# Value products kept together in fours with TensorE's order pinned, and fewer gathers at the ends of the mixings

## The chip, the cores and the metric

One NeuronCore of a Trainium2 chip runs the whole program. Its engines run beside each other, each through its own queue in order: TensorE (PE: matmuls, with its weight loads shown apart as PEld), VectorE (DVE), ScalarE (ACT), GpSimd (POOL) and SyncE (SP). DMAs are issued from the queues of SP, ACT and POOL. The metric is the device time of one execution in microseconds; lower is better.

## The reference

One inference step of a two-layer backbone, on 128 prompt tokens (context) and 256 latent tokens of width 1024, all in float32. A layer is a mixing (windowed attention, a bidirectional mLSTM and a pooling, between two projections) and then PEER, a feed-forward with 16384 experts of one row each, of which every token takes 16 for each of 8 heads:

```python
def trunk_layer(x, mods, p, ctx_kv, mlstm_init, rope_pos):
    h = rmsnorm(x, p['norm1_g']) * (1 + sc1) + sh1
    y, kv, fins = mixing_sublayer(h, p, ctx_kv, mlstm_init, rope_pos)
    x = x + g1 * y
    h = rmsnorm(x, p['norm2_g']) * (1 + sc2) + sh2
    x = x + g2 * peer_ffn(h, p['peer_wq'], p['peer_keys'], p['peer_u'], p['peer_v'])

def peer_ffn(x, w_q, sub_keys, u_table, v_table):
    s = jnp.einsum('thcd,hckd->thck', q, sub_keys).astype(F32)
    top_s, top_i = lax.top_k(s, PEER_TOPK)
    cand = (top_s[:, :, 0, :, None] + top_s[:, :, 1, None, :]).reshape(...)
    best_s, best_p = lax.top_k(cand, PEER_TOPK)
    ...
    a = jax.nn.gelu(jnp.einsum('thkd,td->thk', u_table[eb], xb), approximate=False)
    return jnp.einsum('thk,thkd->td', gb * a, v_table[eb])
```

## The kernel before

**Two ways through the experts.** The 256 latents take PEER densely: for all 16384 experts of a layer the up product, gelu, a weight from the routing, and the down product. The 128 prompt tokens take it sparsely: each token's 128 experts are gathered from memory.

**A layer's stages.** (1) The mixing, whose parts run in an order written out by hand, a string a layer (ORDER0, ORDER1). "route" in it routes the prompt's tokens; from there on their gathers can start. An entry "+n" advances the prompt's experts by n steps, one `next(pr.others)` each. (2) The latents' queries and scores: the normed latents (tile hw, written by VectorE in eight pieces), four groups of query products, and on VectorE the top 16 of each row (L937 to L941). ASKED tells how many of the prompt's steps go among these, by layer. (3) The latents' routing on VectorE, which ends in two index tiles ix for each 128 tokens, and 32 chunks of gate building (G) on VectorE, TensorE and ScalarE. Among these stand 23 dense up products ahead of their turn (L1087), and further steps of the prompt, paced by EARLY. The gates are written to memory and read back in parts (DMA gates<-stage, then G<-gates). (4) Dense.

**Dense.** 64 rounds, each over 256 experts (line 1115 on). A round issues the up product of 23 rounds later (rounds 0 to 40): two loads of 512 KB (tile u), each split into a high and a low half by ScalarE and VectorE, and 48 matmuls into A. Then `weigh` multiplies the round's gelu output with the gates, and `down` loads two tiles v, splits them likewise and issues 24 matmuls into po, the latents' accumulators. All these products are `mm3`: three passes (high x high, high x low, low x high). Loads go through a ring of 4 raw tiles. Then come as many of the prompt's steps as keep an even pace to the last rounds; a round with an up product counts double.

**The prompt's steps.** 259 a layer: 128 for keys, 128 for values, three more since work on a row lags its gather by three steps. A key step gathers one expert row for each token (tile gu, 512 KB, issued by GpSimd, L863), and three steps later VectorE takes the dot product with the tokens in one instruction (L883). A value step gathers two half rows (tile gv, twice 256 KB, L869), and every second value step issues a *four*: four products of 32 columns each, `q` = 0 to 3, into four 32-column groups of one PSUM bank pv (L896). Each is a float32 product, which stands as two instructions, so that a four is 8 instructions. The weights of a four are in a tile wz, which is made anew every 16 fours. Key and value rows share five gather buffers.

**What sets the order.** Python writes the instructions in program order, a scheduler then moves them by its estimates, within their dependences. `behind(m)` pins an instruction: it stays behind what was pinned earlier on its engine, in program order. It adds no wait. Before, pinned are each dot product (L883), the first of the four products of a four, the multiplication in `weigh`, one matmul of each chunk part of the gate build and the routing's transposes.

Of the kernel before, what the change touches and what calls it, by code (L numbers as in the profile page):

```python
# [22 lines left out]
KC = 8  # L23
# [13 lines left out]
ALSO = dict(t="at", q="at")  # L37
NRAW = 4

ORDER0 = "np ns kv c q gate qk ox | &mod1 mod1 mem2 mem0 mem1 att0 pool0 &mod2 att1 att2 pool1 mod2 &next0 mix0 spill norm ask mix1 next0 route +20 +3 +6 +3 +3"  # L40
ORDER1 = "np ns q c gate kv att0 qk ox &mod1 mod1 | mem0 pool0 &mod2 mod2 mix0 norm ask mem1 att1 spill route +5 +15 att2 mem2 pool1 +15 +10 mix1 +4"

BIAS = (1.0, 1.0)
NHI = 4
# [11 lines left out]
          dict(row=("r4", R4), PT=("r4", R4), half="half", P=("P", 2), W=("W", 1), num=("num", 1), hr=("hr", 1), hm=("hm", 1),  # L56
               quarter=("r1", 2)))

ASKED = (14, 0)
LAG = 3  # L60
END = (2, 3)
HEAD = 26.0
# [6 lines left out]
def tile_hybrid_step(ctx: ExitStack, tc: tile.TileContext, I, O):  # L69
# [29 lines left out]
        return t  # L99


    PASSES = ((0, 0), (0, 1), (1, 0))

    def split_into(hi, lo, src):
# [24 lines left out]
        split_into(hi, lo, raw)  # L129
        return hi, lo  # L130

    def mm3(out, a, b, first, last):
        for n, (x, y) in enumerate(PASSES):
            pe.matmul(out, a[x], b[y], start=first and n == 0, stop=last and n == 2, skip_group_check=True)  # L134

    class Room:

# [13 lines left out]
            return t  # L151

    GATH = Room(stay, row=("gath", NGATH), half="half", quarter="half")


    behind = tc.keep_in_program_order


    ident = ld("ident", [P, P], I["c_ident"], cst)
# [19 lines left out]
    def tsl(i):  # L179
        return slice(i * P, (i + 1) * P)  # L180
# [592 lines left out]
    class Prompt:  # L773
# [65 lines left out]
        def experts(self):  # L839
# [7 lines left out]
            for k in range(2 * P + LAG):  # L847
# [33 lines left out]
                if 0 <= j < P:  # L881
                    u = late.pop(j)
                    behind(ve.scalar_tensor_tensor(u, u, 1.0, self.h2n, op0=ALU.mult, op1=ALU.mult, accum_out=dots[:, j:j + 1]))  # L883
                elif j >= P and (j - P) % 2 == 1:
                    r, h = (j - P) // 4, (j - P) // 2 % 2
                    if r % 8 == 0 and h == 0:

                        wz = stay.tile([P, 8, 4, 32], F32, tag="row", bufs=1, name=f"wz{l}{r}")
                        gp.memset(wz, 0.0)
                        flat = wz.rearrange("p r j c -> p (r j c)")  # L890
                        for q in range(4):
                            at = 32 * q + r
                            ve.tensor_copy(flat[:, at:at + 7 * 129 + 1:129], wT[:, at:at + 8])  # L893
                    v = [late.pop(j - 1), late.pop(j)]
                    for q in range(4):
                        m = pe.matmul(self.acc[h][32 * q:32 * q + 32, :], wz[:, r % 8, q, :],  # L896
                                      v[q // 2][:, q % 2 * 512:q % 2 * 512 + 512], start=(r == 0), stop=(r == 31),
                                      skip_group_check=True)
                        if q == 0:
                            behind(m)  # L900
                yield

    def queries(l, most):
# [111 lines left out]
    class Experts:  # L1015
# [56 lines left out]
        def up(self, whole=None):  # L1072
# [7 lines left out]
            for j in range(2):  # L1080
                u = (load_split if whole is None else load_whole)(I["u_T"][l, 2 * bp + j], f"u{l}{bp}{j}")
                out = pa[:, j * 256:(j + 1) * 256]
                for k in range(KC):
                    if whole is None:
                        mm3(out, [t[:, tsl(k)] for t in u], [t[:, k, :] for t in self.hs], k == 0, k == KC - 1)
                    else:
                        pe.matmul(out, u[:, tsl(k)], whole[:, k, :], start=k == 0, stop=k == KC - 1, skip_group_check=True)  # L1087
            gl = self.lay.tile([P, 2, 2 * P], F32, tag="gl", bufs=LOOK[l] - 1, name=f"gl{l}{bp}")
# [13 lines left out]
        def down(self, po, bp, w):  # L1102
# [6 lines left out]
            for i, j in ((0, 0), (0, 1), (1, 0), (1, 1)) if end else ((0, 0), (1, 0), (0, 1), (1, 1)):  # L1109
                for h in range(2):  # L1110
                    mm3(po[i][h], [t[:, j, tsl(i)] for t in w], [t[:, h * 512:(h + 1) * 512] for t in v[j]],
                        bp == 0 and j == 0, end and j == 1)

    def dense(l, ex, p3, po, pr):

# [228 lines left out]
```

## Time and profile before

| | us |
|---|---|
| median of three runs | 2739.42 |
| lowest, highest | 2739.12, 2743.07 |
| the profiled execution | 2746.87 |
| its span | 2745.1 |
| TensorE, VectorE, ScalarE, GpSimd busy in it | 2500.7, 1722.4, 1045.5, 927.6 |
| dense, layer 0 | 683.0 to 1388.0 |
| dense, layer 1 | 2042.1 to 2732.1 |

The profile shows one execution, so its own time, and not the median, is what a sum over its rows is compared with. Busy shares are means over stages that differ much: TensorE is busy 91% of the span and full nearly everywhere in dense, but not at the ends of the scores. The chain of waits follows the work that ended last back to the beginning, and is where to see whether an engine, a transfer or a wait set the time of a stretch. The windows give the busy time of each engine in a stretch, and the DMA share and rate beside it.

### The profile page before, as it was taken

Reading aid. Unit: us, or ns where it says so; the run is one execution under the profiler, and the core shown is the slowest. Engines: PE = TensorE matmul, PEld = TensorE weight load, DVE = VectorE, ACT = ScalarE, POOL = GpSimd, SP = SyncE. Lnnn points to the kernel's source line nnn. Section 1 sums busy time; section 2 is a strip of 40 time slices with the busy share of each in tenths; the row PEclk is TensorE's granted clock in tenths of the full one; section 3 lists DMA queues with packets and bytes.
Section 4 is the critical chain, followed back from the end, with each engine's and each line's share of the span. In section 5 each row is a group of like instructions: output and inputs, shape, how many; then the busy total and the mean of one; then the engine's idle time right before and its main releaser. Section 6 shows DMA issues by size and latency. Waiting matters only on the chain.

```text
span 2745.1 us, 37514 instructions
## 1 busy us (share of the span) xinstructions
PE 2500.7 (91%) x13834; PEld 1915.5 (70%) x13834; DVE 1722.4 (63%) x3768; ACT 1045.5 (38%) x1545; POOL 927.6 (34%) x794
## 2 busy tenths in 40 slices
PE   7998779896999999999989885979969999999998
PEld 3744568785988777765666464868859877777665
DVE  4555979866877444443565468798778844444446
ACT  3434411544434433332444352114444433343333
POOL 0000034101445666754400002231224556656541
PEclk9998989897999999999999878999979999999999
DMA  7485589678899889897835644886999988888985
GB/s 258 139 269 194 167 289 337 210 268 321 305 352 347 303 314 330 290 330 259 292 122 166 218 162 152 315 291 232 334 347 353 329 296 311 299 315 289 330 294 192
DMA packets 217547, 749.33 MB, mean 273 GB/s; under 512 B 28308, under 2 KB 30868, under 8 KB 215316
## 3 DMA queue, kind: packets, MB, share of 16 engines
q1 hardware_dynamic: 137236, 444.91, 46.8%
q0 software_dynamic: 77824, 268.48, 27.9%
q10 hardware_dynamic: 2304, 33.56, 3.1%
q8 instruction: 108, 1.77, 0.3%
q14 instruction: 75, 0.61, 0.1%
HBM read 706.99 MB, written 39.85 MB: 272 GB/s over the span
## 4 chain that ended last, share of the span: by engine, by line
PE 62%; DMA 13%; DVE 12%; issue 7%; POOL 3%; ACT 2%; SPq 0%; POOLq 0%; DVEq 0%; ACTq 0%
PE po L134 22%; PE A L134 13%; PE pv L896 6%; DMA gu<-in_peer_u,ei 4%; PE A L1087 4%; PE pj_i L134 4%; DMA v_r<-in_peer_v 3%; DVE gu L883 3%; DMA gv<-in_v_half,eiT 2%; DMA wm<-in_w_mod 2%; PE pm L305 2%; POOL gu L863 2%; PE pj_t L134 2%; POOL gv L869 2%; PE pj_o L134 1%
## 5 line engine op out<-in xcount | busy, mean ns | idle before, releaser
L869 POOL DMA_INDIRECT gv<-in_v_half,eiT x512 | 590.1, 1153 | 437.7 <-PE pv L896 288.4
L134 PE MATMUL po<-v_h,W 128*128 128x512 f32 x2048 | 668.8, 398 | 30.5 <-ACT W L105 16.0
L863 POOL DMA_INDIRECT gu<-in_peer_u,ei x256 | 324.5, 1267 | 1095.0 <-DVE gu L883 474.6
L134 PEld LDWEIGHTS po<-v_h,W 128*128 128x128 f32 x2048 | 388.8, 191 | 160.7 <-ACT W L105 44.1
L106 DVE TENSOR_TENSOR v_l<-v_r,v_h 128x1024 fp32r<-128x1024 f32 x256 | 313.0, 1224 | 273.7 <-ACT v_h L105 273.5
L134 PE MATMUL A<-hs,u_h 128*128 128x256 f32 x2624 | 482.7, 284 | 1.3 <-ACT u_h L105 0.9
L134 PEld LDWEIGHTS A<-hs,u_h 128*128 128x128 f32 x2624 | 406.8, 189 | 58.9 <-issue 34.4
L105 ACT CAST v_h<-v_r 128x1024 fp32r<-128x1024 f32 x256 | 268.4, 1049 | 385.7 <-PE po L134 155.4
L134 PE MATMUL po<-v_l,W 128*128 128x512 f32 x1024 | 406.0, 397 | 0.1
L134 PE MATMUL A<-hs,u_l 128*128 128x256 f32 x1312 | 370.7, 283 | 2.4 <-DVE u_l L106 2.4
L106 DVE TENSOR_TENSOR u_l<-u_r,u_h 128x1024 fp32r<-128x1024 f32 x164 | 199.1, 1224 | 275.3 <-ACT u_h L105 275.2
L883 DVE SCALAR_TENSOR_TENSOR gu<-gu,h2n 128x1024 f32<-128x1024 f32 x256 | 307.4, 1218 | 63.7 <-DMA gu<-in_peer_u,ei 63.1
L1087 PE MATMUL A<-hw,u_r 128*128 128x256 f32 x1472 | 339.1, 386 | 0.0
L1087 PEld LDWEIGHTS A<-hw,u_r 128*128 128x128 f32 x1472 | 276.5, 193 | 36.0
L105 ACT CAST u_h<-u_r 128x1024 fp32r<-128x1024 f32 x164 | 171.4, 1050 | 307.8 <-PE A L134 258.5
L134 PEld LDWEIGHTS A<-hs,u_l 128*128 128x128 f32 x1312 | 248.3, 189 | 10.9 <-issue 6.7
L134 PEld LDWEIGHTS po<-v_l,W 128*128 128x128 f32 x1024 | 195.6, 191 | 49.6 <-issue 11.7
L896 PE MATMUL pv<-gv,wz 128*32 128x512 f32 x1024 | 194.2, 605 | 5.9 <-DVE wz L893 3.1
L106 DVE TENSOR_TENSOR W<-gl,W 128x512 fp32r<-128x512 f32 x128 | 87.9, 688 | 52.0 <-ACT W L105 51.9
L105 ACT CAST W<-gl 128x512 fp32r<-128x512 f32 x128 | 79.0, 618 | 105.7 <-PE po L134 72.0
L1089 ACT ACTIVATE gl<-A 128x512 f32<-128x512 f32 x128 | 75.5, 595 | 110.9 <-DVE W L106 62.9
L1046 PE MATMUL G<-o,o 128*128 128x128 f16 x1024 | 89.9, 238 | 30.0 <-DVE o L1038 27.6
(424 smaller groups left out, 2982.0 us busy)
## 6 DMA issues: line engine op xcount, KB each, us to landing
u_r<-in_u_T SPq DMA_DIRECT2D x256, 512.0 KB, 5.9
v_r<-in_peer_v SPq DMA_DIRECT2D x256, 512.0 KB, 5.1
wm<-in_w_mod SPq DMA_DIRECT2D x96, 512.0 KB, 5.7
gates<-stage ACTq DMA_DIRECT2D x14, 2048.0 KB, 10.9
G<-gates SPq DMA_DIRECT2D x16, 1792.0 KB, 12.4
w_o_r<-in_w_out SPq DMA_DIRECT2D x32, 512.0 KB, 4.6
w_q_r<-in_w_q SPq DMA_DIRECT2D x32, 512.0 KB, 5.5
w_i_r<-in_w_in SPq DMA_DIRECT2D x24, 512.0 KB, 4.5
```

The source lines that it names most:

```text
L105: ac.copy(hi, src)
L106: ve.tensor_sub(lo, src, hi.bitcast(F32))
L134: pe.matmul(out, a[x], b[y], start=first and n == 0, stop=last and n == 2, skip_group_check=True)
L305: pe.matmul(pm[32 * j:32 * j + 32, :], silu[:, kc, :], w[:, jj * 512:(jj + 1) * 512], start=(kc == 0), stop=(kc == KC - 1), skip_group_che ...
L863: gp.indirect_dma_start(out=t, out_offset=None, in_=I["peer_u"], in_offset=bass.IndirectOffsetOnAxis(ap=ei[:, k:k + 1], axis=0))
L869: gp.indirect_dma_start(out=t[:, j * 512:(j + 1) * 512], out_offset=None, in_=I["v_half"], in_offset=bass.IndirectOffsetOnAxis(ap=eiT[:, h ...
L883: behind(ve.scalar_tensor_tensor(u, u, 1.0, self.h2n, op0=ALU.mult, op1=ALU.mult, accum_out=dots[:, j:j + 1]))
L896: m = pe.matmul(self.acc[h][32 * q:32 * q + 32, :], wz[:, r % 8, q, :], v[q // 2][:, q % 2 * 512:q % 2 * 512 + 512], start=(r == 0), stop= ...
L1046: m = pe.matmul(pg[:, tsl(t)], o2[:, z, :, t0 + t], o1[:, t0 + t, :], start=(z == 0), stop=(z == 1), skip_group_check=True)
L1087: pe.matmul(out, u[:, tsl(k)], whole[:, k, :], start=k == 0, stop=k == KC - 1, skip_group_check=True)
L1089: ac.activation(gl, pa.rearrange("p (j t) -> p j t", j=2), AF.Gelu)
```

## The change

All four products of a four are pinned, where only the first was. The first pass of every product of `down` is pinned, and the first pass at the first k of each dense up product. In the mixings ORDER0 takes 6 steps where it took 35, ORDER1 8 where it took 49; ASKED lets layer 1 take 14 steps among the scores, where it took none. `behind` is defined earlier in the file, so that `mm3` can use it; the lines below shift by two or three (L883 becomes L885, L896 becomes L898, L134 becomes L137).

```diff
-ORDER0 = "... mix1 next0 route +20 +3 +6 +3 +3"
-ORDER1 = "... spill route +5 +15 att2 mem2 pool1 +15 +10 mix1 +4"
+ORDER0 = "... mix1 next0 route +6"
+ORDER1 = "... spill route +3 +3 att2 mem2 pool1 mix1 +2"
...
-ASKED = (14, 0)
+ASKED = (14, 14)
...
-    def mm3(out, a, b, first, last):
+    def mm3(out, a, b, first, last, pin=False):
         for n, (x, y) in enumerate(PASSES):
-            pe.matmul(out, a[x], b[y], start=first and n == 0, stop=last and n == 2, skip_group_check=True)
+            m = pe.matmul(out, a[x], b[y], start=first and n == 0, stop=last and n == 2, skip_group_check=True)
+            if pin and n == 0:
+                behind(m)
...
-                        if q == 0:
-                            behind(m)
+                        behind(m)
...
-                        mm3(out, [t[:, tsl(k)] for t in u], [t[:, k, :] for t in self.hs], k == 0, k == KC - 1)
+                        mm3(out, [t[:, tsl(k)] for t in u], [t[:, k, :] for t in self.hs], k == 0, k == KC - 1, k == 0)
...
-                        bp == 0 and j == 0, end and j == 1)
+                        bp == 0 and j == 0, end and j == 1, True)
```

TensorE, in layer 0's dense, where the up products have ended, before. The names are output, moving input and weights with layer and number: gv086 is the value tile 86 of layer 0, po the latents' accumulator; 32x512 is one product of a four, "x2" two in a row.

```order
L134 MATMUL po011_5189<-v0401_h_10092,W0401_10081 128x512
L896 MATMUL pv00_7282<-gv084_9996,wz016_9393 32x512 x2
L896 MATMUL pv00_7282<-gv085_10003,wz016_9393 32x512 x2
L896 MATMUL pv01_7283<-gv086_10006,wz016_9393 32x512 x2
L134 MATMUL po000_5186<-v0410_h_10150,W0410_10144 128x512
L134 MATMUL po000_5186<-v0410_l_10151,W0410_10144 128x512
L896 MATMUL pv01_7283<-gv087_10013,wz016_9393 32x512
L134 MATMUL po000_5186<-v0410_h_10150,W0411_10145 128x512
L134 MATMUL po001_5187<-v0410_h_10150,W0410_10144 128x512
L896 MATMUL pv01_7283<-gv087_10013,wz016_9393 32x512
L134 MATMUL po001_5187<-v0410_l_10151,W0410_10144 128x512
L134 MATMUL po001_5187<-v0410_h_10150,W0411_10145 128x512
```

After, at the same four:

```order
L137 MATMUL po011_5102<-v0421_h_10177,W0421_10166 128x512
L898 MATMUL pv00_7698<-gv084_10100,wz016_9601 32x512 x2
L898 MATMUL pv00_7698<-gv085_10107,wz016_9601 32x512 x2
L137 MATMUL po000_5099<-v0430_h_10222,W0430_10216 128x512
L137 MATMUL po000_5099<-v0430_l_10223,W0430_10216 128x512
L137 MATMUL po000_5099<-v0430_h_10222,W0431_10217 128x512
L137 MATMUL po001_5100<-v0430_h_10222,W0430_10216 128x512
```

Before, the four of tiles 86 and 87 is cut into three stretches: the two products of gv086, and each of the two of gv087 alone, with matmuls of the next down between them. After, the four of tiles 84 and 85 stands whole between two rounds' downs; that of 86 and 87 stands whole too, behind the next 24 down matmuls, outside these rows.

TensorE, in layer 0's dense, while up products (A) are still issued, before, at the fours of value tiles 28 to 31 (those of 32 to 35 stand inside the next round's up product):

```order
L134 MATMUL po011_5189<-v0251_h_8237,W0251_8226 128x512
L896 MATMUL pv00_7282<-gv028_8138,wz00_7287 32x512 x2
L896 MATMUL pv00_7282<-gv029_8145,wz00_7287 32x512 x2
L896 MATMUL pv01_7283<-gv030_8148,wz00_7287 32x512 x2
L896 MATMUL pv01_7283<-gv031_8155,wz00_7287 32x512 x2
L134 MATMUL A049_8285<-hs00_5176,u0490_h_8288 128x256
```

After, at the four of tiles 30 and 31 and the next two:

```order
L137 MATMUL po011_5102<-v0291_h_8663,W0291_8652 128x512
L898 MATMUL pv01_7699<-gv030_8567,wz00_7807 32x512 x2
L898 MATMUL pv01_7699<-gv031_8574,wz00_7807 32x512 x2
L898 MATMUL pv00_7698<-gv032_8577,wz08_8704 32x512 x2
L898 MATMUL pv00_7698<-gv033_8584,wz08_8704 32x512 x2
L898 MATMUL pv01_7699<-gv034_8691,wz08_8704 32x512 x2
L898 MATMUL pv01_7699<-gv035_8698,wz08_8704 32x512 x2
L137 MATMUL A053_8724<-hs00_5089,u0530_h_8727 128x256
```

Three fours stand in a row after a down product, where before there were two, and the second of the three takes a new weight tile (wz08).

VectorE, layer 0, at the end of the norm (hw) and the start of the top-16 (tv), before:

```order
L225 TENSOR_SCALAR hw0_2969<-pt_h205_2990,A01_1919,B01_1920 128x256
L225 TENSOR_SCALAR hw0_2969<-pt_h206_2994,A01_1919,B01_1920 128x256
L883 SCALAR_TENSOR_TENSOR gu04_2818,dots0_2808<-gu04_2818,h2n0_242 128x1024
L225 TENSOR_SCALAR hw0_2969<-pt_h207_2998,A01_1919,B01_1920 128x256
L883 SCALAR_TENSOR_TENSOR gu05_2821,dots0_2808<-gu05_2821,h2n0_242 128x1024
L883 SCALAR_TENSOR_TENSOR gu06_2824,dots0_2808<-gu06_2824,h2n0_242 128x1024
L883 SCALAR_TENSOR_TENSOR gu07_2827,dots0_2808<-gu07_2827,h2n0_242 128x1024
L883 SCALAR_TENSOR_TENSOR gu08_2830,dots0_2808<-gu08_2830,h2n0_242 128x1024
L883 SCALAR_TENSOR_TENSOR gu09_2833,dots0_2808<-gu09_2833,h2n0_242 128x1024
L883 SCALAR_TENSOR_TENSOR gu010_2836,dots0_2808<-gu010_2836,h2n0_242 128x1024
L883 SCALAR_TENSOR_TENSOR gu011_2839,dots0_2808<-gu011_2839,h2n0_242 128x1024
L883 SCALAR_TENSOR_TENSOR gu012_2842,dots0_2808<-gu012_2842,h2n0_242 128x1024
```

After:

```order
L227 TENSOR_SCALAR hw0_2882<-pt_h204_2899,A01_1919,B01_1920 128x256
L227 TENSOR_SCALAR hw0_2882<-pt_h205_2903,A01_1919,B01_1920 128x256
L227 TENSOR_SCALAR hw0_2882<-pt_h206_2907,A01_1919,B01_1920 128x256
L227 TENSOR_SCALAR hw0_2882<-pt_h207_2911,A01_1919,B01_1920 128x256
L938 MAX tv01_2922<-sc001_2982 128x8 x4
```

Before, a dot product (gu04) stands between the hw pieces shown, another (gu03) between earlier ones, and nine (gu05 to gu013, of which eight are shown) between the last hw and the first top-16. After, the eight hw pieces follow each other, and the first top-16 follows them directly.

In layer 0 the first two up products of dense (A023 and A024), and in layer 1 their like, which stood among the last chunks of the gate build, ahead of the first down, now stand behind the build's last chunk, one ahead of the first down and one behind it.

## Rows read from the trace of the kernel before

**Rows 1.** The page, the chain that ended last: shares of the span by line.

```profile
PE po L134 22%; PE A L134 13%; PE pv L896 6%; DMA gu<-in_peer_u,ei 4%; PE A L1087 4%; PE pj_i L134 4%; DMA v_r<-in_peer_v 3%; DVE gu L883 3%; DMA gv<-in_v_half,eiT 2%; DMA wm<-in_w_mod 2%; PE pm L305 2%; POOL gu L863 2%; PE pj_t L134 2%; POOL gv L869 2%; PE pj_o L134 1%
```

**Rows 2.** The chain in dense, both layers: start us, us, what.

```profile
682.97 13.68 PE po L134 x48
696.64 5.70 PE A L134 x48
...
754.86 18.55 DMA v_r<-in_peer_v
...
884.93 5.46 PE po L134 x24
...
2042.13 13.34 PE po L134 x48
...
2182.27 5.46 PE po L134 x24
```

**Rows 3.** The chain, at value products in layer 0's dense.

```profile
894.76 0.99 PE pv L896 x8
...
1194.70 1.85 PE pv L896 x14
...
1284.45 0.97 PE pv L896 x2
```

**Rows 4.** Windows: us, PE (x), PEld (x), DVE (x), ACT (x), POOL busy (x), PEclk, DMA share, GB/s.

```profile
460.00:480.00 20.00, 17.92 (x84) 15.43 (x82) 19.08 (x87) 0.60 (x1) 9.57 (x9) 1.00 0.95 334
480.00:500.00 20.00, 8.43 (x27) 7.02 (x28) 18.88 (x85) 8.64 (x9) 4.16 (x3) 0.57 0.46 146
...
1820.00:1840.00 20.00, 17.95 (x84) 15.46 (x82) 18.64 (x93) 3.37 (x4) 5.03 (x5) 1.00 0.84 294
1840.00:1860.00 20.00, 5.20 (x15) 4.30 (x16) 19.93 (x92) 7.17 (x8) 4.16 (x4) 0.57 0.36 122
```

**Rows 5.** Windows in dense, same columns: pieces of its first part, then parts.

```profile
710.00:720.00 10.00, 10.00 (x65) 9.05 (x64) 9.38 (x14) 4.74 (x6) 7.08 (x4) 1.00 1.00 369
...
740.00:750.00 10.00, 10.00 (x68) 9.26 (x67) 9.59 (x14) 4.51 (x6) 4.81 (x4) 1.00 0.95 352
...
790.00:800.00 10.00, 10.00 (x68) 9.08 (x66) 7.25 (x8) 4.73 (x5) 2.08 (x3) 1.00 1.03 415
683.00:885.00 202.00, 191.31 (x1178) 172.02 (x1179) 161.59 (x215) 85.91 (x100) 95.71 (x59) 0.97 0.91 334
906.00:1203.00 297.00, 295.52 (x1868) 228.33 (x1867) 131.08 (x137) 111.30 (x128) 192.85 (x163) 1.00 0.89 311
2042.00:2182.00 140.00, 134.94 (x817) 120.58 (x818) 112.08 (x149) 59.76 (x70) 58.80 (x38) 0.96 0.94 346
```

**Rows 6.** Tile gv: instructions (duration ns), idle time before them by cause, landing.

```profile
L869 POOL DMA_INDIRECT gv<-in_v_half,eiT x512: 940/947/2452, 861.5 to 2703.8; - x171
...
  issue: 177.5, 567
  DMA gv<-in_v_half,eiT: 20.8, 44
...
DMA to landing us min/median/max: 3.3/5.6/10.0
```

**Rows 7.** DMA issues from 683 to 900 us: count, median us to landing.

```profile
gu<-in_peer_u,ei POOLq DMA_INDIRECT x52, 8.6
```

**Rows 8.** VectorE's timeline ahead of layer 1's scores: start us, us, instruction.

```profile
1706.96 1.22 DVE L883 SCALAR_TENSOR_TENSOR gu<-gu,h2n 128x1024 f32<-128x1024 f32 x1 [1.31 <-DMA gu<-in_peer_u,ei]
```

**Rows 9.** The chain into layer 0's dense.

```profile
655.31 10.93 DMA gates<-stage
...
666.31 15.17 DMA G<-gates
```

**Rows 10.** TensorE's timeline, the last instruction of each layer's dense.

```profile
1387.65 0.39 PE L134 MATMUL po<-v_h,W 128*128 128x512 f32 x1
...
2731.71 0.39 PE L134 MATMUL po<-v_h,W 128*128 128x512 f32 x1
```

More of the change, by code (lines that the diff above doesn't have):

```diff
@@ L38 @@
 NRAW = 4
-ORDER0 = "np ns kv c q gate qk ox | &mod1 mod1 mem2 mem0 mem1 att0 pool0 &mod2 att1 att2 pool1 mod2 &next0 mix0 spill norm ask mix1 next0 route +20 +3 +6 +3 +3"
-ORDER1 = "np ns q c gate kv att0 qk ox &mod1 mod1 | mem0 pool0 &mod2 mod2 mix0 norm ask mem1 att1 spill route +5 +15 att2 mem2 pool1 +15 +10 mix1 +4"
+ORDER0 = "np ns kv c q gate qk ox | &mod1 mod1 mem2 mem0 mem1 att0 pool0 &mod2 att1 att2 pool1 mod2 &next0 mix0 spill norm ask mix1 next0 route +6"
+ORDER1 = "np ns q c gate kv att0 qk ox &mod1 mod1 | mem0 pool0 &mod2 mod2 mix0 norm ask mem1 att1 spill route +3 +3 att2 mem2 pool1 mix1 +2"
 BIAS = (1.0, 1.0)
@@ L99, in ld @@
         return t
+    behind = tc.keep_in_program_order
     PASSES = ((0, 0), (0, 1), (1, 0))
@@ L153, in tile_hybrid_step @@
     GATH = Room(stay, row=("gath", NGATH), half="half", quarter="half")
-    behind = tc.keep_in_program_order
     ident = ld("ident", [P, P], I["c_ident"], cst)
```

## The prediction

> **What bounds the kernel now.** I read the chain of waits first. Two products of TensorE in the dense stage (po, the latents' value product; A, their up product) alone make 35% of it [rows 1], so time is worth something where TensorE stands still or does work it need not, and only there. Followed through a dense stage, the chain is a plain alternation of 48 up and 24 down matmuls, 5.70 + 5.46 = 11.16 us a round [rows 2]. It breaks in two ways. In the first part of dense it changes to a DMA (the value load, 18.55 us); there seventeen rounds took 884.93 - 682.97 = 201.96 us, 11.88 each, where TensorE alone needs 11.16, and in layer 1 twelve took 140.14, 11.68 each [rows 2]. In the second part it is interrupted by the prompt's value products pv. A whole four (8 instructions) takes 0.99 us, and two instructions standing alone take 0.97; fourteen in a row take 1.85 [rows 3]. The products of a four use four different 32-column groups, and the rows read as if these ran beside each other: the price is for a stretch, not for an instruction.
>
> Then the windows, for stretches where TensorE is idle before dense: 460 to 500 us has 2.08 + 11.57 us of it, 1820 to 1860 us 2.05 + 14.80, while VectorE is busy 37.96 and 38.57 of 40 us [rows 4]. Last the transfers: 334 GB/s at a DMA share of 0.91 in the first part of dense, 311 at 0.89 in the second [rows 5].
>
> **Splits.** By the order of instructions TensorE has 128 fours. Before, 31 are cut by other matmuls, into 54 stretches more than there are fours; after, none. Each extra stretch costs what a lone one shows, so 54 x 0.97 = **-52 us** [rows 3]. All of it lies on the path: po or A goes on at once behind each.
>
> **Waits that the pinning adds.** A pin is no semaphore, but when a gather is late, everything behind the pinned product in TensorE's queue waits with it: the next down and up, and through them the buffers of their loads. After the change nearly every round of dense's second part holds two fours (38 such rounds in both layers), and layer 0 has three rounds with three fours back to back. There are five gather buffers, and the first four of a pair frees two. GpSimd then issues six half gathers, each 0.95 us and 177.5 / 567 = 0.31 of issue [rows 6], so the last starts about 0.2 + 5 x 1.25 = 6.45 us later; the 0.2, for the release, is an estimate below the 0.31 of issue. By the median landing of 5.6 us [rows 6] it is there at 12.05; the next round's second four wants it at 0.97 + 11.16 + 0.97 = 13.1. At 8.6 us, which the other gathers (gu) take in the busiest stretch [rows 7], it would be 1.95 late. I take 7.0, between these two, since the second part's DMA share must rise towards the first's: 0.35 x 38 = 13. That the whole tile waited 20.8 us for gathers in 44 waits before [rows 6], in which pairs stand in the order too, speaks for the low end. The third four of a triple finds no tile filled ahead: 1.25 + 7.0, less the 0.97 of the second four, is 7.3, so 22 for the three. Sum **+35**; bounds 0 (all covered) and, at 8.6, 1.95 x 38 + 3 x 8.9 = 101.
>
> **More gathers in dense.** ORDER0 and ORDER1 put 29 and 41 steps fewer into the mixings, ASKED 14 more into layer 1's scores: net 29 and 27 of a layer's 259 steps move into dense. The rate rises from 3.73 to 4.29 steps a round in layer 0 and from 3.41 to 3.94 in layer 1, and the part with the key gathers (gu) grows from 17.2 to 21.7 rounds and from 13.5 to 18.5. It is the part in which loads are late. A step moves 0.524 MB. Layer 0 moved 334 x 11.88 = 3.97 MB a round and will move 3.97 + 0.56 x 0.524 = 4.26; layer 1 goes from 346 x 11.68 = 4.04 to 4.32. If DMA sets all of it, at the mean rates [rows 5], rounds take 12.75 and 12.48 us; over TensorE's 11.16 that is 1.59 x 21.7 + 1.32 x 18.5 = 59, less the 0.72 x 17 + 0.52 x 12 = 18 lost before: +41. At the rates of these rows scaled to a full share, 334 / 0.91 = 367 and 346 / 0.94 = 368, they take 11.6 and 11.7 us: 0.45 x 21.7 + 0.58 x 18.5 = 20, less 18: about 0. Ten-microsecond rows between show 369 and 352 GB/s at shares of 1.00 and 0.95 [rows 5], but the late loads came all the same, so I take the middle, **+20**. VectorE, busy 161.59 of 202 us there [rows 5], gets 0.56 more dot products of 1.22 us a round: 0.80 + 0.06 = 0.86 busy. At its fullest it is at 9.59 of 10, where this would be late too; I price that at nothing, as a part of the same +20.
>
> The fastest ten microseconds, 790 to 800, reach 415 GB/s [rows 5]. Beside this the Trainium skill ("DMA: Bandwidth & Descriptors", section "Where 436 GB/s comes from") says that between HBM and SBUF the HBM side binds, near 358 GB/s a core. As a hard cap it would make this term +14; the 415 doesn't agree with a cap that low over so short a time.
>
> **Fewer gathers before dense.** A step's dot product holds VectorE 1.22 us [rows 8]. Between the last norm writes (hw) and the first top-16 the order has 11 and 12 of them before, counting those between the hw, and none after; between there and the first chosen indices (ix) 34 and 30 before, 16 and 18 after. So VectorE comes to ix at least 18 x 1.22 = 22 us sooner in layer 0 and 12 x 1.22 = 15 us in layer 1, beside the 11 and 12 ahead of the first top-16, and TensorE's 13.65 and 16.85 us of idle time there [rows 4], in which it waited for ix, goes: -30.5. What is late next is TensorE's own work, so no more is to be had there. Further, on the way into the scores two dot products stand between the hw writes in layer 0, and in layer 1 six more than after before or between them, one behind a wait of 1.31 us [rows 8]: 8 x 1.22 + 1.3 = -11. And the first two dense ups (2 x 5.70 us) stood among the last gate builds, ahead of the gates' way out and back, 10.93 + 15.17 us in which TensorE has nothing to do [rows 9]. After, one stands in that gap and the other behind the first down: both leave the way to dense, one comes back in it, -11.4 in the two layers. The gates' loads on SP's queue stand ahead of two 512 KB loads that they stood behind, worth between 0 and 1.05 MB / 334 = 3 us a layer; I take 0, since those loads are wanted directly after. Sum **-53**; bounds -30 (the idle time alone) and 56 x 1.22 = -68.
>
> **The sum.** -52 + 35 + 20 - 53 = -50 against the profiled execution's 2746.87: 2697. That execution lies 7.45 above the median of the runs, 2739.42, so **2689**.
>
> **Rivals.** All but the last turn on what DMA delivers in dense. The two dense stages take 705 and 690 us, from the first po to the last [rows 2, 10], 1395 together. Their loads and gathers (210 loads of 0.524 MB a layer, 189 and 171 gather steps, 16.8 MB of gates a layer) are 443 MB, 317 GB/s; after, with 56 steps more, 472 MB. My forecast makes dense 1395 - 52 + 35 + 20 + 11 (the two ups) = 1409 us, 335 GB/s.
> *Larger gain:* waits and late loads stay hidden, the two plus terms are 0, -105: **2634**. It needs 472 / 1354 = 349 GB/s, and 311 / 0.89 = 349 is all that the second part's row gives at a full share; for it speaks how little the fours waited before. Chance 0.17.
> *Slower, dense at its present rate:* if gathers wait for buffers, and loads for gathers, so that dense stays at 317 GB/s, it takes 472 / 0.317 = 1488 us, 93 more; -53 and -11 come off before it, so +29: **2769**. It decides below 472 / (1395 + 64) = 324 GB/s. For it: the share is 0.89 to 0.94 already. Against: 346 over 140 us of layer 1 [rows 5]. Chance 0.13.
> *The cure does nothing:* the fours stay whole, but TensorE loses right behind each what it gained. Without the -52: **2741**, the same. The chain's rows in which a whole four costs no more than two lone instructions [rows 3] speak against it. Chance 0.05.
> The forecast has 0.65; with its unknown terms moved one at a time, to +41 for the loads or 0 for the waits, it goes from 2654 to 2710, and with the waits at their upper bound to 2755. The range 2630 to 2740 leaves out the slower case and some of the tails. A measurement can tell some 0.2% (5.5 us) from no change: faster 0.82, same 0.05, slower 0.13.
>
> **What would show it.** Stretches of pv with 8 instructions in 0.97 to 1.00 us, none with 2. No idle TensorE between the scores and the build, so that the first po comes some 27 us earlier in layer 0 (13.65 + 2.4 + 11.4) and 37 more of layer 1's own in layer 1. Three triples with TensorE idle about 7 us behind a gather. A first part of dense of 22 and 18 rounds of nearly 12 us. Wrong would be pairs that wait over 1.5 us each, first-part rounds over 12.5 us, or idle time that stays in the scores because something other than VectorE's queue was late.

## The result, and the profile after

The changed kernel takes 2713.6 us (median of four executions, 2704.45 to 2718.3) against 2739.27: 0.990 of the time before, with a 95% interval of 0.987 to 0.993. Forecast were 2689, and a range of 2630 to 2740. The time got shorter, by half of what was forecast. One execution of spread_cap, below, took 4807 us, a slow run, and is left out of its median.

The profiled execution took 2718.3 us, 28.6 less than the profiled one of before. The page, busy times and the chain (as [rows 1]):

```profile
span 2716.5 us, 37523 instructions
...
PE 2465.0 (91%) x13834; PEld 1917.8 (71%) x13834; DVE 1715.3 (63%) x3768; ACT 1047.2 (39%) x1545; POOL 948.2 (35%) x794
...
PE 56%; DMA 15%; issue 12%; DVE 10%; POOL 5%; ACT 2%; SPq 0%; POOLq 0%; DVEq 0%; ACTq 0%
PE po L137 19%; PE A L137 10%; DMA v_r<-in_peer_v 5%; PE pv L898 4%; PE pj_q L257 4%; PE pj_i L137 4%; DMA gv<-in_v_half,eiT 4%; POOL gv L871 3%; DVE gu L885 2%; PE pm L307 2%; DMA wm<-in_w_mod 2%; PE A L1088 2%; PE pj_o L137 2%; PE pj_t L137 2%; DMA gu<-in_peer_u,ei 1%
```

The two dense products make 29% of the chain where they made 35%, and the value gathers weigh more in it, as DMA (4% where they had 2%) and as GpSimd's work (3% where it had 2%). TensorE is busy 36 us less, and yet the span is only 29 us shorter.

Cut at the first and the last po of each layer, the profiled executions differ so (us):

| | before | after | |
|---|---|---|---|
| to layer 0's first po | 683.0 | 649.2 | -33.8 |
| layer 0's dense | 705.0 | 732.4 | +27.4 |
| from there to layer 1's first po | 654.1 | 629.9 | -24.2 |
| layer 1's dense | 690.0 | 691.7 | +1.7 |

So all of the gain lies ahead of dense, and half of it is given back in layer 0's dense. For dense I added up TensorE's records by tile, each stretch from its first instruction to the next tile's first. Its stretches of pv took 186.2 us before, in 146 stretches, and take 187.4 after, in 83. At 0.97 us for a stretch of one four or less, 1.85 for a pair and 2.8 for a triple these would be 173.3 and 120.3: the pinning took 53 us off, and 54 us more of waits in and between the fours put it on again (13 before, 67 after: 31 at the triples, 28 at the 39 pairs, 7 at lone fours). The po and A stretches together went from 1208 to 1233 us, 11.4 of them for the two ups that moved into dense. The other 14 I put down to later loads: TensorE's idle time ahead of po and A grew from 16 to 31 us.

Where the waits stand is seen in TensorE's timeline at the three triples of layer 0 (start, us, instruction, in brackets the idle time before it and what ended it):

```profile
931.78 2.77 PE L898 MATMUL pv<-gv,wz 128*32 128x512 f32 x20
940.45 3.56 PE L898 MATMUL pv<-gv,wz 128*32 128x512 f32 x4 [5.91 <-DMA gv<-in_v_half,eiT]
...
1037.09 1.06 PE L898 MATMUL pv<-gv,wz 128*32 128x512 f32 x8
1045.34 3.98 PE L898 MATMUL pv<-gv,wz 128*32 128x512 f32 x16 [7.19 <-DVE wz L895]
...
1145.83 1.92 PE L898 MATMUL pv<-gv,wz 128*32 128x512 f32 x16
1159.07 2.24 PE L898 MATMUL pv<-gv,wz 128*32 128x512 f32 x8 [11.32 <-DMA gv<-in_v_half,eiT]
```

The first waits for a gather. The second stops at a new weight tile, and so does the third, though the profile puts it down to a gather, as GpSimd's timeline shows, and VectorE's for the last line:

```profile
1147.19 1.91 POOL L871 DMA_INDIRECT gv<-in_v_half,eiT  x1 [2.48 <-PE pv L898]
1149.40 0.94 POOL L871 DMA_INDIRECT gv<-in_v_half,eiT  x1 [0.30 <-issue]
...
1156.89 0.95 POOL L871 DMA_INDIRECT gv<-in_v_half,eiT  x1 [0.30 <-issue]
1157.84 0.96 POOL L891 MEMSET wz<- 128x1024 f32 x1
```

```profile
1158.84 0.39 DVE L895 COPY wz<-wT 128x8 f32<-128x8 f32 x4 [10.56 <-POOL wz L891]
```

The two fours ahead of the wait freed their buffers, GpSimd issued eight half gathers into them, 1.25 us each but for the first, and only behind these the memset that clears the weight tile for the next sixteen fours. VectorE's copies start 0.04 us behind it, and TensorE 0.2 us after these. Both engines had stood still since 1148. But the weight tile is not the whole of it, for a triple needs six tiles, and there are five buffers. These are the landings of the two half gathers that filled the sixth tile in the second triple (issued at 1038.45 and 1040.66) and in the third (1147.19 and 1149.40):

```profile
DMA to landing us min/median/max: 5.1/5.9/6.7
```

```profile
DMA to landing us min/median/max: 5.0/5.8/6.5
```

The last landed at 1045.8 and 1154.4. So the gathers alone would have held the second triple's last four about as long, and the third's until 4.7 us before it went on at 1159.07.

The wait also costs what comes behind it. Windows of the changed kernel, columns as in [rows 4]:

```profile
936.00:938.00 2.00, 0.00 (x0) 0.00 (x0) 0.00 (x0) 0.00 (x0) 1.39 (x3) 1.00 1.04 386
938.00:940.00 2.00, 0.00 (x0) 0.00 (x0) 0.00 (x0) 0.00 (x0) 1.70 (x2) 0.69 1.03 381
940.00:942.00 2.00, 1.55 (x2) 0.18 (x2) 0.00 (x0) 0.00 (x0) 1.39 (x3) 0.50 1.04 405
942.00:944.00 2.00, 2.00 (x4) 0.24 (x3) 0.00 (x0) 0.00 (x0) 1.51 (x2) 0.50 1.04 400
944.00:946.00 2.00, 2.00 (x12) 2.00 (x12) 0.00 (x0) 0.00 (x0) 1.58 (x2) 0.61 1.02 395
946.00:948.00 2.00, 2.00 (x19) 2.00 (x19) 0.00 (x0) 0.33 (x1) 1.39 (x3) 1.00 1.03 397
```

TensorE stood still from 934.5; its granted clock fell to 0.50 (1.2 GHz) while it did, and was back at 1.00 only by 946. The two products behind the wait (four instructions) took 3.56 us: their half rows had landed at 940.4 and 942.1, and they ran at half the clock. So the three triples lost 9.4, 9.4 and 12.6 us against 2.8 each.

The pairs wait in another way, with hardly any idle time, as this one in layer 1, on TensorE and before that on GpSimd:

```profile
2416.92 2.71 PE L898 MATMUL pv<-gv,wz 128*32 128x512 f32 x12
2419.85 1.04 PE L898 MATMUL pv<-gv,wz 128*32 128x512 f32 x2 [0.23 <-DMA gv<-in_v_half,eiT]
2421.16 1.04 PE L898 MATMUL pv<-gv,wz 128*32 128x512 f32 x2 [0.26 <-DMA gv<-in_v_half,eiT]
```

```profile
2405.08 1.91 POOL L871 DMA_INDIRECT gv<-in_v_half,eiT  x1 [2.48 <-PE pv L898]
...
2409.80 1.93 POOL L871 DMA_INDIRECT gv<-in_v_half,eiT  x1 [0.30 <-issue]
...
2413.28 1.27 POOL L871 DMA_INDIRECT gv<-in_v_half,eiT  x1 [0.30 <-issue]
```

The second four is whole in the order, but its products start one by one as their half rows land, and the last alone holds TensorE for 1.0 us, as long as a whole four. Of the 39 pairs 17 lost 27.6 of the 28 us, and every one of these ended 1.0 us behind the landing of its last half row. By the same rule, and as an estimate, gathers alone, at full clock, would have cost the three triples 8.4, 6.9 and 6.7 us, 22 together; the other 9 are the clock and, in the third, the weight tile.

Ahead of dense the idle time of [rows 4] is gone. The same stretches in layer 0, and in layer 1, which runs 30 us earlier by then, the two ahead of the chosen indices:

```profile
460.00:480.00 20.00, 20.00 (x96) 17.55 (x95) 18.00 (x83) 9.48 (x14) 0.94 (x1) 1.00 0.54 182
480.00:500.00 20.00, 20.00 (x135) 17.78 (x134) 19.00 (x35) 12.41 (x17) 3.03 (x2) 1.00 0.49 158
...
1800.00:1820.00 20.00, 20.00 (x94) 17.60 (x93) 19.93 (x93) 6.57 (x7) 4.15 (x4) 1.00 0.88 313
1820.00:1840.00 20.00, 19.63 (x110) 17.22 (x109) 16.89 (x48) 6.52 (x9) 2.01 (x2) 1.00 0.53 168
```

But in layer 1 something else is late now. The chain of waits into its dense, first before, then after:

```profile
2039.46 0.60 ACT stage L1051
...
2040.74 0.70 DVE gl L1097
...
2042.13 2.93 PE po L134 x6
```

```profile
1989.54 1.73 PE G L1047 x14
...
1991.29 0.35 ACT stage L1052
1991.64 18.36 DMA G<-gates
...
2011.49 8.62 PE po L137 x24
```

Before, the last gate chunk was done at 2040.1, and po followed in 2.0 us. After, the last chunk is done at 1999.9, 11.6 us ahead of po: the gates' way back from memory, which the longer build had covered, ends last.

### The profile page after: what moved, and what is told of

Read it like the earlier page. It is cut to its first block, busy times and chain, and to the rows that moved or that the text cites. A ratio compares the mean times of both kernels' runs of the same rounds, so it can differ in the third digit from the quotient of the medians.

```text
span 2716.5 us, 37523 instructions
## 1 busy us (share of the span) xinstructions
PE 2465.0 (91%) x13834; PEld 1917.8 (71%) x13834; DVE 1715.3 (63%) x3768; ACT 1047.2 (39%) x1545; POOL 948.2 (35%) x794
## 4 chain that ended last, share of the span: by engine, by line
PE 56%; DMA 15%; issue 12%; DVE 10%; POOL 5%; ACT 2%; SPq 0%; POOLq 0%; DVEq 0%; ACTq 0%
PE po L137 19%; PE A L137 10%; DMA v_r<-in_peer_v 5%; PE pv L898 4%; PE pj_q L257 4%; PE pj_i L137 4%; DMA gv<-in_v_half,eiT 4%; POOL gv L871 3%; DVE gu L885 2%; PE pm L307 2%; DMA wm<-in_w_mod 2%; PE A L1088 2%; PE pj_o L137 2%; PE pj_t L137 2%; DMA gu<-in_peer_u,ei 1%
## 5 line engine op out<-in xcount | busy, mean ns | idle before, releaser
L865 POOL DMA_INDIRECT gu<-in_peer_u,ei x256 | 358.0, 1399 | 1157.8 <-DVE gu L885 471.5
L137 PE MATMUL po<-v_h,W 128*128 128x512 f32 x2048 | 670.9, 399 | 38.3 <-ACT v_h L108 17.0
L871 POOL DMA_INDIRECT gv<-in_v_half,eiT x512 | 577.2, 1127 | 326.5 <-PE pv L898 191.3
L137 PEld LDWEIGHTS po<-v_h,W 128*128 128x128 f32 x2048 | 390.1, 191 | 160.9 <-ACT W L108 40.9
L137 PE MATMUL A<-hs,u_h 128*128 128x256 f32 x2624 | 479.0, 284 | 0.4 <-ACT wT L881 0.4
L137 PEld LDWEIGHTS A<-hs,u_h 128*128 128x128 f32 x2624 | 408.9, 190 | 40.6 <-issue 18.4
L137 PE MATMUL po<-v_l,W 128*128 128x512 f32 x1024 | 405.2, 396 | 2.2 <-DVE v_l L109 2.2
L137 PE MATMUL A<-hs,u_l 128*128 128x256 f32 x1312 | 370.6, 283 | 1.6 <-DVE u_l L109 1.6
L1088 PE MATMUL A<-hw,u_r 128*128 128x256 f32 x1472 | 333.6, 382 | 0.0
L885 DVE SCALAR_TENSOR_TENSOR gu<-gu,h2n 128x1024 f32<-128x1024 f32 x256 | 305.5, 1218 | 32.3 <-DMA gu<-in_peer_u,ei 32.2
L137 PEld LDWEIGHTS A<-hs,u_l 128*128 128x128 f32 x1312 | 249.7, 190 | 2.2 <-DVE u_l L109 2.0
L137 PEld LDWEIGHTS po<-v_l,W 128*128 128x128 f32 x1024 | 196.0, 191 | 41.2 <-DVE v_l L109 4.0
L898 PE MATMUL pv<-gv,wz 128*32 128x512 f32 x1024 | 160.6, 616 | 40.6 <-DMA gv<-in_v_half,eiT 24.9
L1047 PEld LDWEIGHTS <-o 128*128 128x128 f16 x1024 | 84.5, 150 | 46.2 <-DVE o L1039 39.8
```

The source lines that it names most:

```text
L137: m = pe.matmul(out, a[x], b[y], start=first and n == 0, stop=last and n == 2, skip_group_check=True)
L865: gp.indirect_dma_start(out=t, out_offset=None, in_=I["peer_u"], in_offset=bass.IndirectOffsetOnAxis(ap=ei[:, k:k + 1], axis=0))
L871: gp.indirect_dma_start(out=t[:, j * 512:(j + 1) * 512], out_offset=None, in_=I["v_half"], in_offset=bass.IndirectOffsetOnAxis(ap=eiT[:, h ...
L1047: m = pe.matmul(pg[:, tsl(t)], o2[:, z, :, t0 + t], o1[:, t0 + t, :], start=(z == 0), stop=(z == 1), skip_group_check=True)
```

## The experiments

Each was compared with the kernel before on its own chip; the ratio is to that, with its 95% interval. "pv" is the sum of TensorE's stretches of value products in the profile, as above.

| kernel | median us | ratio | pv, us (stretches) |
|---|---|---|---|
| changed kernel | 2713.6 | 0.990 (0.987 to 0.993) | 187.4 (83) |
| pins_only | 2712.3 | 0.987 (0.982 to 0.992) | 161.8 (89) |
| orders_only | 2853.6 | 1.042 (1.039 to 1.046) | 307.1 (274) |
| cap2 | 2690.0 | 0.983 (0.979 to 0.986) | 179.7 (83) |
| spread | 2682.7 | 0.980 (0.977 to 0.983) | 148.0 (123) |
| pins_spread | 2710.5 | 0.988 (0.986 to 0.990) | 130.2 (128) |
| spread_cap | 2687.3 | 0.981 (0.979 to 0.984) | 148.7 (123) |
| gate_early | 2711.2 | 0.988 (0.986 to 0.990) | 192.7 (83) |
| spread_gate | 2678.2 | 0.979 (0.975 to 0.983) | 148.3 (123) |
| five_21 | 2723.7 | 0.995 (0.991 to 0.999) | 194.7 (83) |
| six_21 | 2680.2 | 0.977 (0.975 to 0.980) | 148.0 (83) |
| thirds_gate | 2676.5 | 0.975 (0.972 to 0.978) | 135.1 (128) |
| six_gate_cap | 2682.1 | 0.978 (0.975 to 0.981) | 142.9 (84) |

**The change in two halves.** pins_only has the new pins and the old numbers:

```diff
-ORDER0 = "... route +6"
+ORDER0 = "... route +20 +3 +6 +3 +3"
-ORDER1 = "... route +3 +3 att2 mem2 pool1 mix1 +2"
+ORDER1 = "... route +5 +15 att2 mem2 pool1 +15 +10 mix1 +4"
-ASKED = (14, 14)
+ASKED = (14, 0)
```

> The pins alone (all four products of a four, the downs' first passes, the dense ups' first), with the mixings' strings and ASKED as before. By the order of instructions the fours stand in 89 stretches, 50 single and 39 pairs, none split, no triple; before there were 146. Theory (the pins' gain is eaten by waits for gathers): at 0.97 us for a lone stretch and 1.85 for a pair the stretches cost 121 us instead of 169, -48; a pair waits about 1 us (the pairs of the changed kernel lost some 35 us in 36), +35 less the 17 us that the fours of before lost already: net -31, about 2708 us, first po of both layers where it was. Rival 1 (the pins gain nothing, all of the change's gain is ahead of dense): 2739. Rival 2 (pairs wait no more than before): -48, 2691.

It took 2712.3, near the theory's 2708 and level with the whole change. The fours' stretches fell by 24 us, not by the 53 that fewer stretches are worth: pairs wait. Dense as a whole took only 7.5 us less than before (1387.5 against 1395.0). What was not expected is that most of the gain lies ahead of dense: the first po came 8.6 us earlier, and layer 1's own part was 14.7 shorter. One up product stands there ahead of the first down, where before there were two; I put it down to that. orders_only has the new numbers and the old pins (`if q == 0: behind(m)`, no pin in `mm3`):

> The strings and ASKED alone, without the new pins. By the order of instructions the fours now stand in 274 stretches, 128 more than before, most of them one or two products long. Theory (a stretch costs 0.97 us whatever it holds): +124 in dense, about +19 for the longer first part and the two ups that come back into it +11; ahead of dense -34 and -24 as in the changed kernel: about 2739 + 96 = 2835. Rival (lone products slip into gaps that TensorE has anyway, the earlier dense is what counts): 2739 - 58 + 30 = 2711, as the whole change.

It took 2853.6, above the theory's 2835 and far from the rival. Its first po stands at 651.0 us, where that of the changed kernel stands, and its own part of layer 1 took 624.4: the gain ahead of dense needs no pins. But its dense took 816.5 and 741.0 us. TensorE's timeline there shows why, in the middle of an up product:

```profile
1003.91 1.05 PE L896 MATMUL pv<-gv,wz 128*32 128x512 f32 x2
1004.89 0.51 PE L134 MATMUL A<-hs,u_h 128*128 128x256 f32 x2
...
1006.40 1.05 PE L896 MATMUL pv<-gv,wz 128*32 128x512 f32 x4
...
1008.05 1.04 PE L896 MATMUL pv<-gv,wz 128*32 128x512 f32 x2
```

One product or two cost what a whole four costs, and with the later gathers the scheduler cuts far more of them: 274 stretches, 307.1 us. This is the price of a split shown by itself: 121 us for 128 stretches more, of which 112 by the prices above and 9 as longer waits. It also tells which pins do the work: with all four products of a four pinned but not the downs and ups, the order on TensorE is that of orders_only row by row. A pin holds only against other pinned instructions.

So ahead of dense the two halves overlap: the strings and ASKED take 62 us off there by themselves, the pins 23, both together 58. Beside the pins the strings and ASKED are worth 35 us there, and with the fours in pairs all of that is lost again in dense (1387.5 to 1424.1): pins_only 2712.3, with them 2713.6.

**Triples.** cap2 allows two fours a round. In the code `want` is the count of steps that the pace asks for by the end of a round, `pr.done` those that are done; from P + LAG on they are value steps, and `span[bp]` is 2 in a round that has an up product:

```diff
+            if pr.done >= P + LAG:
+                want = min(want, pr.done + 4)
             while pr.done < want:
```

> The changed kernel with at most two fours a round (four of the prompt's steps): by the order the three triples of layer 0 become pairs, all else is as it was. Theory (a third four finds no filled buffer, and TensorE's clock falls in the wait): the triples' stretches lost 9.4 + 9.4 + 12.6 = 31 us against 2.8 each; nearly all of it goes, pairs in their place lose about 1 each: -28, 2686 us. Rival (dense is bound by what the DMA moves, the waits are only where that shows): the loads are late instead, 2714.

2690.0, near the theory's 2686, but only half of it in the way that the theory says. In the profile, which is 31 us shorter, layer 0's dense is 717.5 us instead of 732.4. The rest lies ahead of dense (643.3 and 618.0 us), and executions of kernels with the same strings differ that much there: 618.0 to 632.5 us for layer 1's own part in eight profiles. The triples' share is shown by dense alone, 15 us. The fours' stretches fell by 8 us only: the late steps wait in the tail instead, in pairs of up to 8.5 us.

**Pairs.** spread puts one four behind the up and one behind the down:

```diff
             ex.up()
+            if pr.done >= P + LAG and span[bp] == 2:
+                while pr.done < want - 2:
+                    next(pr.others)
             w = ex.weigh(p3, bp)
```

> The changed kernel with the pair pulled apart: in rounds that have an up product, one four stands behind the up and one behind the down; by the order 118 single stretches and 5 pairs. Theory (a pair waits since five buffers don't hold what two fours and the steps between want): gathers have two spans of 5.5 us instead of one of 11.2, the 67 us that the fours lost in the changed kernel shrink to 10, 40 more stretches cost 0.1 each: -53, 2661 us. Rival (DMA-bound dense): 472 MB then have to move at 345 GB/s; if the rate stays at 331 as in the changed kernel, the time stays at 2714 and the waits turn into waits for loads.

2682.7, between the two theories. The fours' stretches fell by 39 us, po and A took 10 more. The mean rate in dense is 472 MB / 1394.5 us = 338 GB/s, above the 331 of the changed kernel, so the rate had not been the limit; but a quarter of what the fours no longer waited came back as late loads. spread_cap (both edits) and pins_spread (both, with the old strings) followed:

> spread with at most two fours a round: by the order the pairs of layer 0's main part become single stretches, four pairs stand where the up products have ended. Theory (any two fours in a row may wait for gathers): the pairs and what followed them lost some 16 us in layer 0's dense (stretches of 3.6, 10.3 and 3.4 us, a down of 10.1), about 8 come back at the four pairs in the tail: -8, 2675. Rival (loads set the pace, the place of the fours matters no more): 2683.

> The pins with the mixings' strings and ASKED of before, and the pairs pulled apart as in spread, at most two fours a round; by the order 128 single stretches. It tells what fewer gathers ahead of dense are worth when the fours no longer wait. From the profiles: ahead of dense pins_only took 674 + 639 us, spread 646 + 623, 44 less; in dense pins_only took 699 + 688, of which the fours' stretches 162; single ones cost 128 x 0.97 = 124, and a quarter of that gain came back as late loads in spread: -28. Theory (fewer gathers ahead come back almost wholly in dense): 2712 - 28 = 2684, level with spread's 2683. Rival 1 (they are worth the 44 us they save ahead of dense): 2683 + 44 = 2727. Rival 2 (dense with 56 gathers fewer is so much the freer): 2670.

spread_cap took 2687.3: not faster than spread, and the 4.6 us more are less than single executions of either differ. Its four pairs in the tail lost 2.4, 1.4, 2.8 and 10.7 us. pins_spread gained nothing over pins_only (2710.5), although its dense took 27 us less in the profile (685.8 + 674.7 against 699.4 + 688.2): layer 1's own part took 666.5 us where that of pins_only took 639.4, and I can't say why. Against spread it is 28 us slower, against spread_cap, which differs from it by the strings and ASKED alone, 23. So fewer gathers ahead are worth 20 to 30 us where the fours don't stand in pairs, between the theory (nothing) and the first rival (44), as far as that stretch of layer 1 isn't chance.

**Buffers.** six_21 has six gather buffers, for which there is room with 21 up products ahead; five_21 is its control, with the same order of fours on TensorE.

```diff
-NMORE = 2
+NMORE = 3
...
-LOOK = (23, 23)
+LOOK = (21, 21)
```

> The changed kernel with 21 up products ahead of their turn instead of 23, as the control for six_21 (room for a sixth gather buffer is only there with 21). By the order two triples and 41 pairs, the same fours as in six_21. Each theory: two up products a layer move from the build, where TensorE does them in 12 us, into dense, where they take 11.4; one triple fewer: 2714 - 10 = 2704, with pairs and triples waiting as in the changed kernel.

> five_21 with six gather buffers instead of five, the fours in the same order. Theory (a pair waits because five buffers can't hold its four tiles and those of the next): with six, both tiles of a pair's second four are asked for a four earlier; waits of pairs and triples shrink from some 55 us to 15, a quarter of it comes back as late loads: 30 below five_21. Rival 1 (gathers are late since GpSimd issues them at 1.25 us a half row, or since they land late beside the loads): the same as five_21. Rival 2 (more gathers under way delay the loads more): slower than five_21.

The sixth buffer is worth 43 us, 2723.7 to 2680.2. The views by tile, who waited for gv (us, times), first five_21, then six_21:

```profile
  POOL gv L871: 218.4, 92
  PEld pv L898: 42.1, 39
```

```profile
  POOL gv L871: 129.1, 77
  PEld pv L898: 10.7, 19
```

GpSimd waits 89 us less for products to free a tile, TensorE's weight loads 31 us less for gathers. The same gathers, beside the same loads: it was the buffers, not the rate of issue or the landing. What six_21 still loses stands at the weight tiles; TensorE's timeline of it:

```profile
2317.35 1.07 PE L898 MATMUL pv<-gv,wz 128*32 128x512 f32 x8
2323.11 2.24 PE L898 MATMUL pv<-gv,wz 128*32 128x512 f32 x8 [4.69 <-DVE wz L895]
```

five_21 was 10 us slower than the changed kernel where 10 faster was expected. Its pairs in layer 1 straddle two renewals of the weight tile, each a wait as this one, with 8.6 us lost each; no pair in the changed kernel's layer 1 lost more than 3.4.

**The gates.** gate_early reads six of the first gates' seven parts one part of the build earlier:

```diff
+            if early:
+                sy.dma_start(g[:, 0:NS - 2], self.spilled[0:NS - 2, :, rows, :].rearrange("b p r t -> p b r t"))
+                return
...
-            if c == (NS - 1) * per:
+            if c == (NS - 2) * per:
                 self.gates(p3, 0, early=True)
+            if c == (NS - 1) * per:
+                sy.dma_start(self.G[0][:, NS - 2], self.spilled[NS - 2, :, 0:2 * PG, :])
```

> The changed kernel, only the first gates' way back is cut differently: six of the seven parts that come from memory are read one part earlier, and behind the seventh only that one (256 KB instead of 1.8 MB). Theory (after the change it is the gates' way out and back that ends last ahead of dense, not TensorE: the last chunk's output is done at 637.7 and 1999.9, the first down starts at 649.2 and 2011.5): the first down comes 5 to 7 us sooner in each layer, never before the last chunk and the gelu product behind it, 1.4 us: -12, 2702. Rival (the chunk's matmuls and the up product in the gap hold TensorE anyway): 2714.

> spread_cap and gate_early together. Theory: they lie in different places and add up: 2675 - 12 = 2663. Rival (the earlier read meets the dense loads or the build's own writes): 2675 or more.

From the last chunk to po it now takes 6.1 and 6.3 us instead of 11.5 and 11.6, and that is one up product. But the last chunk came 3 us later in both layers, and by the medians 2 us are left, less than these runs tell from nothing: 2711.2 is the rival's time, not the theory's 2702. With spread_cap's edit (spread_gate) it is 9 us faster than spread_cap, less than single executions of either differ, and again the rival's time, not the theory's 2663.

**What is best.** thirds_gate is gate_early with every four alone: one behind the up, one behind the down, and a third in the middle of the down (`until(n)` does steps until n are done).

```diff
...
+            values = pr.done >= P + LAG
+            many = want - pr.done > 4
+            if values and span[bp] == 2:
+                until(want - 4 if many else want - 2)
             w = ex.weigh(p3, bp)
-            ex.down(po, bp, w)
+            ex.down(po, bp, w, lambda: until(want - 2) if values and (many or span[bp] == 1 and want - pr.done > 2) else None)
+            until(want)
```

> gate_early's read of the gates, with every four on its own: in dense's second part one behind the up, one behind the down, and where a round has three, the third in the middle of the down; by the order 128 single stretches. Theory (what the fours still lost in spread, 24 us, hangs on the two-four stretches and what follows them): 12 of it goes, and the earlier gates give 5 to 8: 2683 - 18 = 2665. Rival (the rest is late loads, not the fours' places): 2678, as spread_gate.

> Six gather buffers and 21 up products ahead, with the earlier read of the gates and at most two fours a round: the three remedies that lie in different places. Theory (they add up): six_21's 2680, less 5 to 8 for the gates, less 6 for the two triples that six_21 still has, with half of that back where the tail catches up: 2670. Rival (with six buffers triples wait little, and the loads take up what is left): 2680.

thirds_gate is the fastest by its median, 2676.5, 63 us below the kernel before and 37 below the change, but its interval overlaps those of spread_gate, six_21 and six_gate_cap; it is the rival's time, not the theory's 2665, though the fours' stretches fell from 148 to 135 us. The edits of six_gate_cap did not add up: 2682.1, where six_21 alone took 2680.2. All kernels with the new strings whose fours seldom wait for buffers end between 2676 and 2687. What thirds_gate still loses at its fours is the weight tile, as here, with eight half gathers ahead of the memset on GpSimd:

```profile
1135.14 2.24 PE L898 MATMUL pv<-gv,wz 128*32 128x512 f32 x8 [5.64 <-DVE wz L895]
```

That the memset's place in GpSimd's queue is the cause is read from the timelines. It was not tried to clear the tile elsewhere, or to have two.

## Why the prediction was right, and where its sum was off

**The splits** (-52): right. The stretches without their waits went from 173.3 to 120.3 us, -53, and orders_only shows the price the other way.

**The waits** (+35): too small by 19, and the term that failed most. The fours lost 13 us before and 67 after, +54. The pairs lost 28 where 13 were forecast. The step that failed there is the issue of the gathers, not their landing: the last of six half gathers was put 6.45 us behind the four that frees the buffers, which leaves it 5.7 us ahead of the next pair. In 14 of the 17 pairs that waited it was issued 3.6 us ahead; in the pair shown two of the six took 1.9 us where 0.95 was counted. The landing of 7.0 us was rather too long, 5.6 at the median between 926 and 1210 us. So the buffers, which six_21 shows to be the cause, were in the argument, but with a slack of a microsecond that the pairs didn't have.

The triples lost 31 where 22 were forecast. The gathers' part was sized well, 22 by the estimate above; what was left out is the rest: the granted clock falls in a wait, so that 7.19 us of standing still cost 9.4, and the third triple's weight tile came later still. I had listed the edits' effect on GpSimd's queue by its gathers and left out its other instruction, the memset, though [rows 6] give the 1.25 us that stand ahead of it, eight times over. Lone fours lost 7 us that the sum didn't have. Against all this the waits of before, 13 us, were taken as none, which hides that pairs waited there too: taken off, they would have left 22 of the 35.

**More gathers in dense** (+20): 14 by the po and A stretches, within its bounds, and beside it the 11 of the two ups, as forecast. In the first part the DMA share rose to 0.95 and 0.96, and the rate to 353 and 357 GB/s (as [rows 5]):

```profile
649.00:926.00 277.00, 257.45 (x1585) 228.79 (x1586) 229.48 (x312) 115.64 (x135) 141.77 (x95) 0.96 0.95 353
926.00:1210.00 284.00, 256.38 (x1611) 195.67 (x1610) 113.58 (x124) 94.62 (x109) 178.95 (x156) 0.95 0.86 298
2011.00:2231.00 220.00, 209.60 (x1298) 188.44 (x1299) 187.04 (x251) 94.68 (x110) 113.23 (x71) 0.96 0.96 357
```

In layer 0's second part it fell to 298, with TensorE standing still: the waits slow the loads, not the other way round. With the pairs pulled apart (spread) that part moves 321:

```profile
920.00:1200.00 280.00, 267.77 (x1670) 201.97 (x1669) 123.08 (x132) 102.15 (x117) 195.25 (x167) 0.98 0.90 321
```

One step of the working was wrong: the first round of before had no up product in either layer, so the time lost before was 30 us and not 18, and the term by its own rule some 11 lower. The first parts themselves took 277.1 us for 22 rounds and 219.3 for 18. The 12.6 us a round in layer 0 are a little above the 12.5 that I had named as a sign of being wrong, the 12.2 in layer 1 below it; over 11.16 us the two lost 50 us, 20 more than before.

**Fewer gathers ahead of dense** (-53, and 11 that come back): -58 by the first po, against -64. The idle time went whole. The first po came 34 us earlier in layer 0 (27 forecast), where the gates' trip was also shorter, and 24 in layer 1's own part (37 forecast). The failed step is "what is late next is TensorE's own work": it was the gates' way back, 18.36 us, as the chain above shows.

**The sum** by its terms as measured: -53 + 54 + 14 + 11 - 58 = -32, against -28.6 in the profiled executions; 2.7 us of the rest are a wait at the small transpose of the dots in layer 1. The direction was right for what lies ahead of dense. Dense itself, forecast at 1409 us, took 1424, and that is where most of the rest of the gain went.

**The rivals.** The larger gain didn't come. Dense did go beyond its rate of before, 331 against 317 GB/s, so the slower rival's condition was not met. The cure that does nothing was nearest to what happened to the fours, for a reason it didn't name: all that the pinning gained, the waits took.

## What to carry to other kernels

Where instructions are pinned together, work out what the group wants at once: buffers, and every other instruction on the queues that fill them, down to a memset. Price a wait of TensorE with the clock that it loses, and put a gain at nothing until the next late thing behind it has been looked for in the chain of the stage. And place small groups apart rather than pair them, unless being apart costs more than the waits: here a four by itself costs 0.1 us more than one in a pair, and a pair that waits lost one to ten.

## What the runs showed that I had not expected

The granted clock fell to 0.50 in a stand of 6 us and took until 946, over 5 us after work began again at 940.45, to come back. With the same numbers in the mixings, the part from layer 1's start to its first po took 618.0 to 632.5 us in eight profiles, which is about the width that the medians of these kernels are uncertain by. And a profile's "who ended the wait" can name a gather where another cause ended it: the last half row that the third triple needed had landed 4.7 us before TensorE went on, and the end of the 11.32 us put down to a gather was the weight tile's.
